# The opening stage of a two-layer diffusion trunk, in a new order: squares summed on DVE, five parts' modulation by rows of weights, seven product chains by parts and one at the end

## The chip, the cores and the metric

The kernel runs on one core of a Trainium2 chip, in float32 throughout; matrix products use float32r operands split into a high and a low part. The metric is the device time of one launch in microseconds (us), the median of several runs. "PE" is TensorE, "DVE" VectorE, "ACT" ScalarE, "POOL" GpSimd and "SP" the engine that issues most loads.

## The reference

Two layers over 256 latent tokens and 256 context tokens of width 1024. Each sub-layer first normalises and modulates with a shift and a scale that come from the conditioning vectors; the first is a SwiGLU over all 512 tokens:

```
silu_c, silu_cc = silu(c), silu(c_ctx)
m  = silu_c  @ w_mod[0] + b_mod[0]          # 9 x 1024: shift, scale, gate, ...
mc = silu_cc @ w_mod[0] + b_mod[0]          # the same for context tokens
h  = rms_norm(x, g) * (1 + scale) + shift
x  = x + 0.5 * gate * ((silu(a) * b) @ w2),   a, b = split(h @ w13)
... token mixing (attention and pooling), SwiGLU, layer 2: SwiGLU, gMLP, SwiGLU
```

Only the part up to `h @ w13` of the first SwiGLU is touched here.

## The kernel before

Everything is stored transposed: a tile has 128 features on partitions and tokens along the columns. `X` holds 8 parts of 128 features (k = 0 to 7), each 512 columns: 256 latent tokens, then 256 context tokens. A product in full precision is `mm3`: three matmuls, low weights with the high activations `AH`, high weights with `AH`, high weights with `AL`. `split` makes the pair: ACT casts the high part, DVE subtracts to get the low one.

The opening is `start()`. It runs the first four of the SwiGLU's 22 blocks of hidden features (f = 0 to 3, each with halves a and b, so eight chains in eight PSUM banks) part by part: for one part k, all eight chains get their three products, 8 x 3 x 8 = 192 products in all. So they can begin when one part is normalised and its weights are there, long before all modulation vectors are known. After it `ffn` goes on with block 4, whose weights come by `load_w`, whole blocks at a time.

For part k the kernel needs shift and scale of that part for both token kinds. They come in two ways:
- by reduction: a tile `wm` (128x1024, 0.5 MB) of transposed weights is multiplied on DVE with the broadcast conditioning vector `cc` and summed along the columns (`use_mod`, line L80); two tiles and two token kinds make four reductions a part; `finish_mod` adds the bias and makes `gs` = gain x (1 + scale);
- by rows: TensorE multiplies the conditioning columns with plain weight rows (`by_rows`, L697) into a row of results, ACT copies it, and narrow matmuls (L704) turn it into columns. Before the change the last `NR` = 3 parts go this way, all three in one block ahead of the first product.

The parts are taken in the order 0, 5, 1, 6, 2, 7, 3, 4. Part 0's four reductions come first; parts 1 to 4 are reduced beside the products.

Also in the opening, before: `cc` is made by 16 matmuls of a broadcast column with the identity (L665), copied by ACT (L667). The mean square of each token is summed on TensorE: ACT squares a part (L679), a matmul with `ones` adds it (L680), ACT takes the root (L681) and DVE the reciprocal of all 512 columns at once (L685), then `sa` = X times it (L721), ACT applies scale and shift (L724), and `split` makes `AH` and `AL`.

The tile framework sorts instructions of each engine by its own priorities, except those that are pinned with `tc.keep_in_program_order`; each engine runs its list strictly in order. SP's queue of loads is a list of the same kind. A tile name with `bufs=n` has n buffers, and a load into one waits until its last reader is through.

Of the kernel before, what the change touches and what calls it, by code (L numbers as in the profile page):

```python
# [16 lines left out]
P = 128  # L17
D = 1024
# [4 lines left out]
NH = NF // 2  # L23
EPS = 1e-6
NMOD = 72
NR = 3
WINDOWS = (2, 4, 8, 16)
ATTN_SCALE = 0.125

# [6 lines left out]
def trunk(ctx: ExitStack, tc: tile.TileContext, I, out):  # L36
# [47 lines left out]
    def finish_mod(layer, j, n=1, ks=slice(0, NK)):  # L84
# [7 lines left out]
        V.tensor_tensor(out=m, in0=m, in1=b.broadcast_to([P, ns, n, nk]), op=ALU.add)  # L92
        sub, kind = (j + n - 1) // 3, (j + n - 1) % 3
        last = m[:, :, n - 1]
        if kind == 1:
            g0 = C_NG + (layer * 3 + sub) * NK
            g = par[:, g0 + ks.start:g0 + ks.stop].unsqueeze(1).broadcast_to([P, ns, nk])
            V.scalar_tensor_tensor(out=gs[:, st, sub, ks], in0=last, scalar=1.0, in1=g,
                                   op0=ALU.add, op1=ALU.mult)
        if kind == 2:  # L100
            V.tensor_scalar(gate[:, st, sub, ks], last, 1.0 if j == 5 else 0.5, None, ALU.mult)
# [20 lines left out]
            run_mods(1)  # L122


    def load_w(src, n, pin=lambda ins: ins):
# [3 lines left out]
        nc.sync.dma_start(out=raw[:, :n], in_=src)  # L129
# [85 lines left out]
    def ffn(fi, layer, sub, n, mods, after, started=()):  # L215

        defer = n == T
        with tc.tile_pool(name=f"ffn{fi}", bufs=1) as fp:
            HH = fp.tile([P, NH, 2 * T], F32R, name="HH")
            HL = fp.tile([P, NH, 2 * T], F32R, name="HL")  # L220
            for half in range(2):
                hc = half * T if n == T else 0
                for fl in range(NH):
# [1 line left out]
                    if f < len(started):  # L225
                        ps = started[f]
                    else:
                        hi, lo = load_w(I["w13"][fi, f], 2048)
# [409 lines left out]

    def start():
        ng = 4  # L640
        order = (0, 5, 1, 6, 2, 7, 3, 4)
        with tc.tile_pool(name="start", bufs=1) as sp:
            def get_raw(k):
                raw = sp.tile([P, ng, 2 * P], F32, name="raw4", bufs=2)
                nc.sync.dma_start(out=raw, in_=I["w13"][0, 0:ng, :, k * 2 * P:(k + 1) * 2 * P]
                                  .rearrange("f p c -> p f c"))
                return raw

            cT = sp.tile([P, 2, NK], F32, name="cT")
            nc.sync.dma_start(out=cT, in_=I["cT"])  # L650
            nc.sync.dma_start(out=ident, in_=I["ident"])
            wm = {(0, 0): load_mod(0, 0, nc.sync)}
            for k in range(0, NK, 2):
                nc.sync.dma_start(out=X[:, k:k + 2], in_=I["xc"][:, k:k + 2])
            wm[0, 1] = load_mod(0, 1, nc.sync)
            S.activation(out=cT, in_=cT, func=AF.Silu)

            S.activation(out=rb[:, 0:1], in_=cT[:, 0, 0:1], func=AF.Sqrt, scale=0.0, bias=epsb)

            for st in range(2):  # L660
                for h in range(2):
                    ps = bank()
                    for k4 in range(4):
                        k = 4 * h + k4
                        PE.matmul(ps[:, k4 * P:k4 * P + P], cT[:, st, k:k + 1].broadcast_to([P, P]),  # L665
                                  ident, start=True, stop=True)
                    S.copy(cc[:, st, h * 512:h * 512 + 512], ps)  # L667
            nc.sync.dma_start(out=par, in_=I["par"])
            wn = [wpool.tile([P, 2, 2 * NR * P], F32, name=n, bufs=3 if i > 1 else 2)
                  for i, n in enumerate(("raw", "raw", "whi", "wlo"))]  # L670
            for i in range(4):
                nc.sync.dma_start(out=wn[i], in_=I["w_modr"][:, 2 * i:2 * i + 2])
            raws = {0: get_raw(0)}
            wm.update({(1, h): load_mod(0, 2 + h, nc.sync) for h in range(2)})
            raws[order[1]] = get_raw(order[1])
            ps = bank()
            for k in range(NK):
                sq = tmp.tile([P, 2 * T], F32, name="sq", bufs=2)
                S.activation(out=sq, in_=X[:, k], func=AF.Square)  # L679
                PE.matmul(ps, ones, sq, start=k == 0, stop=k == NK - 1)  # L680
            S.activation(out=rb, in_=ps, func=AF.Sqrt, scale=1.0 / D, bias=epsb)  # L681
            for h in range(2):
                use_mod(0, h, wm[0, h])
            finish_mod(0, 0, 2, slice(0, 1))
            V.reciprocal(rb, rb)  # L685
            sh = sp.tile([P, NK, ng - 2, 2 * P], F32R, name="sh")
            sl = sp.tile([P, NK, ng - 2, 2 * P], F32R, name="sl")
            wh, wl = ([wpool.tile([P, NK, 2 * P], F32R, name=n, bufs=3) for _ in range(2)]
                      for n in ("whi", "wlo"))

            def by_rows():

                row = sp.tile([2, 2 * NR * P], F32, name="row")
                ps = [bank() for _ in range(2)]
                for k in range(NK):
                    for j in range(2):
                        PE.matmul(ps[j][0:2, :NR * P], cT[:, :, k],  # L697
                                  wn[k // 2][:, k % 2, j * NR * P:(j + 1) * NR * P],
                                  start=k == 0, stop=k == NK - 1)
                for j in range(2):  # L700
                    S.copy(row[:, j * NR * P:(j + 1) * NR * P], ps[j][0:2, :NR * P])
                ps = bank()
                for i in range(2 * NR):
                    PE.matmul(ps[:, 2 * i:2 * i + 2], row[:, i * P:i * P + P], ident[0:2, 0:2],  # L704
                              start=True, stop=True)
                for st in range(2):
                    V.tensor_copy(mod[:, st, :16].rearrange("p (j k) -> p j k", j=2)[:, :, NK - NR:],
                                  ps[:, 0:4 * NR].rearrange("p (j k s) -> p s j k", j=2, k=NR)[:, st])
                finish_mod(0, 0, 2, slice(NK - NR, NK))

            by_rows()
            pss = [[bank(), bank()] for _ in range(ng)]
            nxt = 1
            for i, k in enumerate(order):
                raw = raws.get(k) or get_raw(k)
                split(sh[:, k], sl[:, k], raw[:, :2])
                split(wh[0][:, k], wl[0][:, k], raw[:, 2])
                split(wh[1][:, k], wl[1][:, k], raw[:, 3])
                xr = tmp.tile([P, 2 * T], F32, name="sa", bufs=2)
                h = tmp.tile([P, 2 * T], F32, name="h32", bufs=2)  # L720
                V.tensor_tensor(out=xr, in0=X[:, k], in1=rb, op=ALU.mult)  # L721
                for st in range(2):
                    ts = slice(st * T, st * T + T)
                    S.activation(out=h[:, ts], in_=xr[:, ts], func=AF.Identity,  # L724
                                 scale=gs[:, st, 0, k:k + 1], bias=mod[:, st, k:k + 1])
                if nxt < NK - NR and i in (0, 2, 4, 5):
                    for j in range(2):
                        use_mod(0, 2 * nxt + j, wm.get((nxt, j)) or
                                load_mod(0, 2 * nxt + j, nc.sync), tc.keep_in_program_order)
                    finish_mod(0, 0, 2, slice(nxt, nxt + 1))  # L730
                    nxt += 1
                split(AH[:, k, :2 * T], AL[:, k, :2 * T], h)

                def products(f, k, first, last):
                    for ab in range(2):
                        cs = slice(ab * P, ab * P + P)
                        w = (sh[:, k, f, cs], sl[:, k, f, cs]) if f < 2 else \
                            (wh[f - 2][:, k, cs], wl[f - 2][:, k, cs])
                        mm3(pss[f][ab], *w, AH[:, k, :2 * T], AL[:, k, :2 * T], first, last)

                for f in range(ng):
                    products(f, k, i == 0, i == NK - 1)
        return pss


# [14 lines left out]
def _pack(x, c, ctx, c_ctx, w_mod, b_mod, norm_g, ffn_w13, ffn_w2, w_in_a, qk_norm_g, pool_w,  # L760
# [5 lines left out]
    r["cT"] = ac(np.stack([c[0], c_ctx]).reshape(2, NK, P).transpose(2, 0, 1))  # L766
    r["w_modr"] = ac(w_mod[0][:, :2 * D].reshape(NK, P, 2, NK, P)[:, :, :, NK - NR:]
                     .transpose(1, 0, 2, 3, 4)).reshape(P, NK, 2 * NR * P)
# [70 lines left out]
```

## Time and profile before

| | us |
|---|---|
| runs | 1141.17, 1141.91, 1142.41; median 1141.91 |
| the profiled execution | 1142.17, of it the span of the core 1140.4 |
| TensorE busy | 1132.2 (99% of the span), 7696 matmul passes |
| DVE / ACT busy | 863.6 / 522.0 |
| TensorE busy in the first 27.8 us | 24.49, before the first product |

In the rows that are shown below, a timeline row is: start, duration, engine, line, operation, output<-inputs, shape, count, and in brackets the engine's idle time before it with what ended it. A row of waits is: who waited for whom, us in total, times, longest. A row of groups ends with busy us, mean ns of one, and idle time before. A row of a stretch is: from:to, length, then busy us and count for PE, weight loads, DVE, ACT and POOL (or PE alone), the granted clock of TensorE, the DMA engines' share and GB/s. A row of one source line gives count, minimum, median and maximum in ns, first and last start, and the forms with their counts.

### The profile page before, as it was taken

What the parts mean: (1) busy time and instruction counts of PE and PEld (TensorE: products, weight loads), DVE (VectorE), ACT (ScalarE), POOL (GpSimd) and SP (SyncE); (2) the same over time, 40 slices, a digit from 0 to 9 for tenths busy, and PEclk for the clock granted to TensorE, in tenths of its full rate; (3) what the DMA queues carried; (4) which work ended last, traced back from release to release, by engine and by line L of the source; (5) the groups of instructions that cost most, each with busy time, mean ns of one, the idle gap of its engine ahead of it and who ended that gap; (6) DMA issues with size and microseconds to landing.
All of it is one profiled execution on the core that took longest, in us unless ns stands there. A gap on an engine that the chain in (4) does not pass through costs nothing.

```text
span 1140.4 us, 19165 instructions
## 1 busy us (share of the span) xinstructions
PE 1132.2 (99%) x7696; PEld 1033.9 (91%) x7696; DVE 863.6 (76%) x1582; ACT 522.0 (46%) x816; POOL 68.4 (6%) x140
## 2 busy tenths in 40 slices
PE   8999999999999999999999999999999999999998
PEld 4888888888888897899999999999999899999998
DVE  5967787878789979777778887656667788756663
ACT  5552212223223357664335456435445866434442
POOL 0000111122222200000000000000000000000000
PEclk9999999999999999999999999999999999999999
DMA  8844656788888850556687566456447536546543
GB/s 323 310 148 156 197 186 234 279 282 325 294 297 306 305 196 11 222 172 223 212 305 264 187 219 218 161 167 219 174 143 257 185 114 219 176 154 237 178 143 114
DMA packets 52408, 242.72 MB, mean 213 GB/s; under 512 B 5600, under 2 KB 11488, under 8 KB 38880
## 3 DMA queue, kind: packets, MB, share of 16 engines
q1 hardware_dynamic: 33888, 174.39, 43.4%
q0 software_dynamic: 18432, 67.12, 17.4%
q8 instruction: 60, 0.98, 0.4%
q14 instruction: 28, 0.23, 0.1%
HBM read 240.44 MB, written 1.05 MB: 212 GB/s over the span
## 4 chain that ended last, share of the span: by engine, by line
PE 97%; DVE 1%; ACT 1%; DMA 1%; issue 0%; SPq 0%; DVEq 0%; ACTq 0%
PE ps L148 30%; PE ps L149 30%; PE ps L150 30%; PE ps L697 1%; PE ps L618 1%; PE ps L619 1%; PE ps L617 1%; PE ps L680 1%; PE ps L665 1%; DMA raw<-in_w_out_a 0%; ACT whi L153 0%; PE ps L501 0%; PE ps L469 0%; DVE st L473 0%; PE ps L172 0%; ACT pe L477 0%
## 5 line engine op out<-in xcount | busy, mean ns | idle before, releaser
L148 PE MATMUL ps<-AH,wlo 128*128 128x258 f32 (+2 forms) x1664 | 507.1, 305 | 0.3 <-ACT AH L153 0.3
L149 PE MATMUL ps<-AH,whi 128*128 128x258 f32 (+2 forms) x1664 | 506.6, 305 | 0.0
L150 PE MATMUL ps<-AL,whi 128*128 128x258 f32 (+2 forms) x1664 | 505.5, 305 | 0.0
L153 ACT CAST whi<-raw 128x1024 fp32r<-128x1024 f32 (+2 forms) x354 | 313.7, 921 | 363.7 <-PE ps L150 260.3
L154 DVE TENSOR_TENSOR wlo<-raw,whi 128x1024 fp32r<-128x1024 f32 (+2 forms) x354 | 367.6, 1064 | 54.4 <-ACT whi L153 53.4
L148 PEld LDWEIGHTS ps<-AH,wlo 128*128 128x128 f32 x1664 | 316.3, 190 | 16.1 <-issue 1.1
L149 PEld LDWEIGHTS ps<-AH,whi 128*128 128x128 f32 x1664 | 314.3, 189 | 14.7 <-issue 0.5
L150 PEld LDWEIGHTS ps<-AL,whi 128*128 128x128 f32 x1664 | 313.4, 189 | 14.5 <-issue 0.2
L150 PE MATMUL ps<-HL,whi 128*128 128x256 f32 (+1 forms) x704 | 218.0, 310 | 0.0
L149 PE MATMUL ps<-HH,whi 128*128 128x256 f32 (+1 forms) x704 | 218.0, 310 | 0.0
L148 PE MATMUL ps<-HH,wlo 128*128 128x256 f32 (+1 forms) x704 | 218.0, 310 | 0.0
L80 DVE CUSTOM_DVE_ANT_0 wm<-wm,cc 128x1024 f32<-128x1024 f32 x138 | 164.7, 1219 | 6.1 <-DMA wm<-in_w_mod 5.0
L148 PEld LDWEIGHTS ps<-HH,wlo 128*128 128x128 f32 x704 | 132.5, 188 | 7.8
L150 PEld LDWEIGHTS ps<-HL,whi 128*128 128x128 f32 x704 | 132.5, 188 | 7.7
L149 PEld LDWEIGHTS ps<-HH,whi 128*128 128x128 f32 x704 | 132.6, 188 | 7.7
L72 POOL DMA_DIRECT2D wm<-in_w_mod x128 | 67.7, 529 | 546.2 <-DVE mod L80 508.6
L206 ACT ACTIVATE sa<-sa,cb 128x256 f32<-128x256 f32 x66 | 33.6, 510 | 119.7 <-DVE sa L205 116.4
L246 DVE SCALAR_TENSOR_TENSOR X<-ps,gate,X 128x256 f32<-128x256 f32 x64 | 30.9, 482 | 48.0 <-PE ps L150 47.9
L204 DVE COPY cb<-ps 128x1 f32<-128x1 f32 x66 | 10.3, 155 | 72.8 <-PE ps L150 72.7
L212 DVE TENSOR_TENSOR h<-ps,sa 128x512 f32<-128x512 f32 x22 | 15.2, 692 | 43.4 <-PE ps L150 34.2
L80 DVE CUSTOM_DVE_ANT_0 junk<-wm,cc 128x1024 bf16<-128x1024 f32 x34 | 41.4, 1218 | 8.6 <-ACT cc L667 7.2
L154 DVE TENSOR_TENSOR HL<-h,HH 128x256 fp32r<-128x256 f32 (+1 forms) x88 | 42.3, 485 | 0.0
(162 smaller groups left out, 705.3 us busy)
## 6 DMA issues: line engine op xcount, KB each, us to landing
raw<-in_w SPq DMA_DIRECT2D x84, 1024.0 KB, 4.9
wm<-in_w_mod POOLq DMA_DIRECT2D x128, 512.0 KB, 5.0
raw<-in_w SPq DMA_DIRECT2D x64, 704.0 KB, 4.1
wm<-in_w_mod SPq DMA_DIRECT2D x10, 512.0 KB, 6.4
raw<-in_w_in_a SPq DMA_DIRECT2D x5, 1024.0 KB, 7.8
raw<-in_w SPq DMA_DIRECT2D x8, 512.0 KB, 5.3
raw<-in_w_out_a SPq DMA_DIRECT2D x4, 1024.0 KB, 5.0
raw<-in_w_in_cu SPq DMA_DIRECT2D x4, 1024.0 KB, 4.8
```

Of the source, the lines that this page charges most:

```text
L72: eng.dma_start(out=w, in_=I["w_mod"][layer, i])
L80: pin(V.tensor_tensor_reduce(out=res, in0=w, in1=cc[:, st, :], scale=1.0, scalar=0.0, op0=ALU.mult, op1=ALU.add, accum_out=mod[:, 2 * laye ...
L148: PE.matmul(ps, wl, xh, start=first, stop=False)
L149: PE.matmul(ps, wh, xh, start=False, stop=False)
L150: PE.matmul(ps, wh, xl, start=False, stop=last)
L153: S.copy(hi, src)
L154: pin(V.tensor_tensor(out=lo, in0=src, in1=hi.bitcast(F32), op=ALU.subtract))
L206: S.activation(out=sa[:, :T], in_=sa[:, :T], func=AF.Silu, bias=cb[:, 0:1])
L212: V.tensor_tensor(out=h32[:, :n], in0=ps[1][:, :n], in1=sa[:, :n], op=ALU.mult)
L246: V.scalar_tensor_tensor(out=X[:, m, :T], in0=ps[:, :T], scalar=gate[:, 2 * layer, sub, m:m + 1], in1=X[:, m, :T], op0=ALU.mult, op1=ALU.add)
L617: PE.matmul(ps[b], AL[:, k, ts], hi[:, ws], start=(k == 0), stop=False)
L618: PE.matmul(ps[b], AH[:, k, ts], hi[:, ws], start=False, stop=False)
```

## The change

Only the opening changes, and with it the packing of its inputs.
- The conditioning columns, with a small selector `sel`, come in one load `cs`; X is loaded first, in five pieces, with `wm` behind it. All loads of the opening are pinned in program order.
- `cc`: DVE multiplies the identity with the broadcast columns into a diagonal tile, and four 512-column matmuls with `ones` spread it; DVE copies one token kind's half, ACT the other's.
- Squares: ACT squares, DVE adds them into `acc` (`square_acc`), and two 256-column matmuls with `ones` sum over partitions at the end. Root and reciprocal are made by token half.
- The queue: a one-column ACT copy into the next rows' buffer makes SP hold that load, and all behind it, until ACT has come to part 5 of X.
- By rows now go five parts, `ROWS` = 3 to 7, one at a time: 8 matmuls with 32 stationary columns (2 real, the others zero) in four column groups of the array, partitions 32g to 32g + 31 of the bank; a row copy; two narrow matmuls with `sel`, which also add the four groups up. The first block stands ahead of the products, the others between the products of the part before.
- The order is 3, 4, 0, 5, 1, 6, 2, 7. Parts 0, 1 and 2 are reduced on DVE, one part ahead. The first part is done in token halves of 256 columns.
- Seven chains go by parts; the eighth (f = 3, half b) is done for all parts at the end, since the rows need a bank.
- `load_w` pins the loads of blocks 4 and 5. `raw4` has three buffers in place of two.

```diff
+ROWS = (3, 4, 5, 6, 7)
...
-        order = (0, 5, 1, 6, 2, 7, 3, 4)
+        order = (3, 4, 0, 5, 1, 6, 2, 7)
+        jobs = {1: 0, 2: 1, 4: 2}
...
+            diag = cc.rearrange("p s (k c) -> p s k c", k=NK)
+            bc = [bank() for _ in range(4)]
             for st in range(2):
+                V.tensor_tensor(out=diag[:, st], in0=ident.unsqueeze(1).broadcast_to([P, NK, P]),
+                                in1=c32[:, :, st:st + 1].broadcast_to([P, NK, P]), op=ALU.mult)
                 for h in range(2):
-                    ps = bank()
-                    for k4 in range(4):
-                        k = 4 * h + k4
-                        PE.matmul(ps[:, k4 * P:k4 * P + P], cT[:, st, k:k + 1].broadcast_to([P, P]),
-                                  ident, start=True, stop=True)
-                    S.copy(cc[:, st, h * 512:h * 512 + 512], ps)
+                    PE.matmul(bc[2 * st + h], ones, diag[:, st, 4 * h:4 * h + 4],
+                              start=True, stop=True)
...
+            for k in range(NK):
+                square_acc(k, 2 * T)
+                if k in (4, 5):
+                    V.tensor_copy(cc[:, 0, k % 2 * 512:k % 2 * 512 + 512], bc[k - 4])
+                if k == 5:
+                    pin(S.copy(rows[4][:, 0, 0:1], X[:, k, 0:1]))
+            for st in range(2):
+                ts = slice(st * T, st * T + T)
+                PE.matmul(ps[:, ts], ones, acc[:, ts], start=True, stop=True)
...
+            def by_rows(k):
+                w = rows.pop(k)
+                for kt in range(NK):
+                    g = kt % 4
+                    pin(PE.matmul(rw[32 * g:32 * g + 32, :2 * P], c32[:, kt], w[:, kt],
+                                  start=kt < 4, stop=kt >= 4))
+                row = sp.tile([P, 2 * P], F32, name="row", bufs=2)
+                pin(S.copy(row, rw[:, :2 * P]))
+                for j in range(2):
+                    PE.matmul(rw[:, 2 * P + 2 * j:2 * P + 2 * j + 2], row[:, j * P:j * P + P], sel,
+                              start=True, stop=True)
+                finish_mod(0, 0, 2, slice(k, k + 1),
+                           rw[:, 2 * P:2 * P + 4].rearrange("p (j s) -> p s j", j=2).unsqueeze(3))
...
+                if i == 0:
+                    for ts in halves:
+                        if ts.start:
+                            pin(V.reciprocal(rb[:, ts], rb[:, ts]))
+                            subs(pin)
+                            rest(halves[0])
+                        pin(V.tensor_tensor(out=xr[:, ts], in0=X[:, k, ts], in1=rb[:, ts],
+                                            op=ALU.mult))
+                        if ts.start == 0:
+                            casts(pin)
+                        normed(ts, AH[:, k, ts])
+                        normed(ts, h[:, ts])
+                    rest(halves[1])
...
+                else:
+                    for f, ab in todo:
+                        if ahead is not None and (f, ab) == (1, 0):
+                            by_rows(ahead)
+                        mm3(pss[f][ab], *tile(f, ab), AH[:, k, :2 * T], AL[:, k, :2 * T], False,
+                            i == NK - 1)
             ps = bank()
             for k in range(NK):
...
+                mm3(ps, *tile(ng - 1, 1, k), AH[:, k, :2 * T], AL[:, k, :2 * T], k == 0, k == NK - 1)
```

The built order shows it at three places. In its rows ISA is a reduction (L80 before, L81 after) and the short read that follows it; `sl` and `wlo` are low weights, `AL` low activations, and the numbers on `raw` and `h` tell parts apart. First DVE, from the reciprocal to the first low parts. Before:

```order
L685 RECIPROCAL rb<-rb 128x512
L721 TENSOR_TENSOR sa<-X,rb 128x512 x3
L154 TENSOR_TENSOR AL<-h_227,AH 128x512
L154 TENSOR_TENSOR sl<-raw_131,sh 128x512
L154 TENSOR_TENSOR wlo<-raw_131,whi 128x256 x2
```

The reciprocal was one operation of 512 columns, with all three low parts behind it. Now, on the same engine:

```order
L722 RECIPROCAL rb<-rb 128x256
L93 TENSOR_TENSOR mod<-ps,par 128x2x2
L100 SCALAR_TENSOR_TENSOR gs<-mod,par 128x2
L782 TENSOR_TENSOR sa<-X,rb 128x256
L779 RECIPROCAL rb<-rb 128x256
L764 TENSOR_TENSOR sl<-raw_97,sh 128x512
L764 TENSOR_TENSOR wlo<-raw_97,whi 128x256 x2
L772 TENSOR_TENSOR AL<-h_188,AH 128x256
```

The second half's reciprocal and the weights' subtractions now stand ahead of the first half's `AL`. Second, DVE beside the first products. Before, from the first part's weights on:

```order
L154 TENSOR_TENSOR wlo<-raw_131,whi 128x256 x2
L80 ISA junk,mod<-wm,cc 128x1024
L80 ISA mod 128x1
L80 ISA wm,mod<-wm,cc 128x1024
L80 ISA mod 128x1
L707 COPY mod<-ps 128x2x3 x2
L80 ISA junk,mod<-wm,cc 128x1024
L80 ISA mod 128x1
L92 TENSOR_TENSOR mod<-mod,par 128x2x2x3
L154 TENSOR_TENSOR sl<-raw_137,sh 128x512
```

The reductions there are those of part 1, the third in its order. Now, from the low activations of part 0, the third part, to `gs` of part 5, the fourth:

```order
L156 TENSOR_TENSOR AL<-h_313,AH 128x512
L81 ISA junk,mod<-wm,cc 128x1024
L81 ISA mod 128x1
L81 ISA wm,mod<-wm,cc 128x1024
L81 ISA mod 128x1
L81 ISA junk,mod<-wm,cc 128x1024
L81 ISA mod 128x1
L93 TENSOR_TENSOR mod<-ps,par 128x2x2
L81 ISA wm,mod<-wm,cc 128x1024
L81 ISA mod 128x1
L100 SCALAR_TENSOR_TENSOR gs<-mod,par 128x2
L764 TENSOR_TENSOR sl<-raw_204,sh 128x512
```

`gs` of part 5 stands behind all four reductions of part 1. (The four reductions of part 0 stand in the same way between `AL` of part 4 and `gs` of part 0.) Third TensorE. Before, the start of the products:

```order
L680 MATMUL ps<-sq,ones 128x512 x8
L697 MATMUL ps<-raw,cT 2x384 x8
L697 MATMUL ps<-whi,cT 2x384 x4
L697 MATMUL ps<-wlo,cT 2x384 x4
L704 MATMUL ps<-ident,row 128x2 x3
L148 MATMUL ps<-AH,sl 128x512
```

All rows (L697) stood ahead of the first product. Now (`c_99` is the 32-column conditioning tile, L730 the rows' matmuls, L735 the narrow ones, L825 the products in halves):

```order
L710 MATMUL ps<-acc,ones 128x256 x2
L730 MATMUL ps<-raw,c_99 32x256 x8
L735 MATMUL ps<-cs,row 128x2 x2
L825 MATMUL ps<-AH,sh 128x256 x4
L825 MATMUL ps<-AH,whi 128x256 x3
L825 MATMUL ps<-AL,sh 128x256 x4
L825 MATMUL ps<-AL,whi 128x256 x3
L825 MATMUL ps<-AH,sl 128x256 x4
L825 MATMUL ps<-AH,wlo 128x256 x3
L730 MATMUL ps<-raw,c_99 32x256 x8
L825 MATMUL ps<-AH,sh 128x256 x4
L735 MATMUL ps<-cs,row 128x2 x2
```

One rows block is ahead of the products and the next already between them.

More of the change, by code (lines that the diff above doesn't have):

```diff
@@ L128, in load_w @@
         lo = wpool.tile([P, 2048], F32R, name="wlo", bufs=3)
-        nc.sync.dma_start(out=raw[:, :n], in_=src)
+        dma_pin(nc.sync.dma_start(out=raw[:, :n], in_=src))
         for c in (slice(0, n // 2), slice(n // 2, n)):
@@ L646, in get_raw @@
                                   .rearrange("f p c -> p f c"))
                 return raw
[L649 to L656, printed above, removed]
@@ new lines, in start @@
+            sync = InOrder(nc.sync)
+            cs = sp.tile([P, 2 * NK + 2], F32, name="cs")
+            sync.dma_start(out=cs, in_=I["cs"])
+            sel = cs[:, 2 * NK:]
+            sync.dma_start(out=ident, in_=I["ident"])
+            for ks in (slice(0, 2), slice(2, 4), slice(4, 6), slice(6, 7), slice(7, 8)):
+                sync.dma_start(out=X[:, ks], in_=I["xc"][:, ks])
+            sync.dma_start(out=par, in_=I["par"])
+            rows, raws, wm = {}, {}, {}
+            get_rows(3)
@@ L671, in start @@
[L671 to L675, printed above, removed]
+                    PE.matmul(bc[2 * st + h], ones, diag[:, st, 4 * h:4 * h + 4],
+                              start=True, stop=True)
+            ps = bank()
+            rw = bank()
+            pin = tc.keep_in_program_order
@@ new lines, in start @@
+            get_rows(4, load=False)
+            for k in range(NK):
[7 more added lines that the diff above has]
+                PE.matmul(ps[:, ts], ones, acc[:, ts], start=True, stop=True)
+            for st in range(2):
+                ts = slice(st * T, st * T + T)
+                pin(S.activation(out=rb[:, ts], in_=ps[:, ts], func=AF.Sqrt, scale=1.0 / D,
+                                 bias=epsb))
@@ L676, in start @@
             ps = bank()
             for k in range(NK):
[L678 to L742, printed above, removed]
```

113 lines of the change are left out of this document (99 added, 14 removed).

## The prediction

> **What bounds the kernel now.** First the share of the chain of work that ended last, then TensorE's own waits over the whole span, then three stretches: up to the first product, the opening's products, and the stretch after them.
>
> ```profile
> PE 97%; DVE 1%; ACT 1%; DMA 1%; issue 0%; SPq 0%; DVEq 0%; ACTq 0%
> ```
> ```profile
> PE ps L665 <- DMA ident<-in_ident: 3.3, 1, 3.3
> PE ps L501 <- ACT pt L493: 0.9, 2, 0.5
> PE ps L469 <- ACT wm L153: 0.4, 1, 0.4
> PE ps L148 <- ACT AH L153: 0.3, 1, 0.3
> ```
> ```profile
> 0.00:27.80 27.80, 24.49 (x86) 11.75 (x86) 15.12 (x24) 14.87 (x26) 0.20 (x4) 1.00 0.86 323
> 27.80:73.40 45.60, 45.60 (x200) 36.94 (x201) 38.63 (x80) 26.40 (x52) 2.24 (x4) 1.00 0.71 245
> 73.40:151.00 77.60, 77.60 (x337) 62.88 (x336) 57.95 (x86) 23.15 (x32) 6.87 (x13) 1.00 0.53 177
> ```
>
> TensorE is the bound: it carries 97% of the chain and waits under 5 us in 1140. From 27.8 us on it is busy without a break (third number of a row). So the change is worth exactly what it does to one instant: when TensorE has done the opening's 192 products of 512 columns and the six narrow ones beside them (the 200 of the second row, within the window's edges) and starts the first product of block 4. Whatever is earlier or later there is passed on to the end, because no later stretch has slack on TensorE. The timeline of TensorE gives that instant and what stands ahead of the products:
>
> ```profile
> 3.31 6.15 PE L665 MATMUL ps<-ident,cT 128*128 128x128 f32 x32 [3.31 <-DMA ident<-in_ident]
> 9.30 7.42 PE L680 MATMUL ps<-sq,ones 128*128 128x512 f32 x16
> 16.65 5.32 PE L697 MATMUL ps<-raw,cT 128*2 128x384 f32 x16
> 27.06 0.82 PE L704 MATMUL ps<-ident,row 2*128 2x2 f32 x6
> 27.82 0.50 PE L148 MATMUL ps<-AH,sl 128*128 128x512 f32 x1
> ...
> 73.07 0.39 PE L150 MATMUL ps<-AL,whi 128*128 128x512 f32 x1
> 73.30 0.40 PE L148 MATMUL ps<-AH,wlo 128*128 128x512 f32 x1
> ```
>
> Products begin at 27.82 and block 4 at 73.30; a product takes 0.23 from start to start, so 192 are 44.5. An f32 matmul is two passes: L697's 32 passes (16 of them in this row) of 384 columns go (27.06 - 16.65)/32 = 0.325 us apart, so a pass of 256 columns is 0.217. 27.82 is nearly all TensorE's own preparatory work, and this the change cuts. The sum is made against the profiled execution (1142.17 us, span 1140.4) and carried over to the median, 1141.91, which is 0.26 lower.
>
> **Step 1: up to the first product.** What X allows is read from the queue, since SP issues its next load when a piece of X has landed, and by equal bytes: after cT and ident the old queue has 0.52 MB of wm before X, the new one starts with X.
>
> ```profile
> 8.92 0.33 SPq L672 DMA_DIRECT2D wlo<-in_w_modr  x1
> 10.15 0.38 SPq L645 DMA_DIRECT2D raw<-in_w  x1
> ```
> ```profile
> 12.73 1.22 DVE L80 CUSTOM_DVE_ANT_0 junk<-wm,cc 128x1024 bf16<-128x1024 f32 x1 [1.38 <-DMA wm<-in_w_mod]
> ```
>
> wm and two pieces had landed by 8.92, so X's third piece now lands about then, the last (2.1 MB) at 10.15. With X, wm twice: 3.15 MB by 12.73; the first rows (1.05 MB behind X and par) land near 13. The queue's hold waits for ACT to reach part 5 of X, at about 10.1, when 1.6 MB are still queued, so it leaves no gap. The costs of single instructions come from the groups of the first 75 us, and from two lines for the 256-column forms:
>
> ```profile
> L724 ACT ACTIVATE h<-sa,mod,gs 128x256 f32<-128x256 f32 x16 | 8.9, 595 | 9.4 <-DVE sa L721 6.8 <-DVE gs L98 2.4
> L153 ACT CAST AH<-h 128x512 fp32r<-128x512 f32 x8 | 5.0, 620 | 0.2
> L679 ACT ACTIVATE sq<-X 128x512 f32<-128x512 f32 x8 | 4.9, 628 | 2.3 <-PE ps L680 1.7 <-DMA X<-in_xc 0.6
> L667 ACT COPY cc<-ps 128x512 f32<-128x512 f32 x4 | 2.3, 581 | 1.6 <-PE ps L665 1.6
> L92 DVE TENSOR_TENSOR mod<-mod,par 128x4 f32<-128x4 f32 x5 | 0.8, 160 | 0.0
> L98 DVE SCALAR_TENSOR_TENSOR gs<-mod,par 128x2 f32<-128x2 f32 x5 | 0.8, 156 | 0.0
> ```
> ```profile
> L173 ACT ACTIVATE rb<-ps,epsb x5: 474/476/690, 410.7 to 952.7; 128x256 f32<-128x256 f32 x4, 128x512 f32<-128x512 f32 x1
> L174 DVE RECIPROCAL rb<-rb x5: 1753/1754/3353, 411.4 to 953.2; 128x256 f32<-128x256 f32 x4, 128x512 f32<-128x512 f32 x1
> L504 ACT COPY hn<-ps x4: 365/373/419, 451.2 to 468.6; 128x256 f32<-128x256 f32 x4
> ```
> ```profile
> 23.98 0.68 DVE L154 TENSOR_TENSOR sl<-raw,sh 128x512 fp32r<-128x512 f32 x1
> 24.58 0.75 DVE L154 TENSOR_TENSOR wlo<-raw,whi 128x256 fp32r<-128x256 f32 x2
> 25.25 1.22 DVE L80 CUSTOM_DVE_ANT_0 junk<-wm,cc 128x1024 bf16<-128x1024 f32 x1
> 26.39 0.08 DVE L80 DVE_READ_ACCUMULATOR2_ANT mod<- 128x1 f32 x1
> 26.51 1.23 DVE L80 CUSTOM_DVE_ANT_0 wm<-wm,cc 128x1024 f32<-128x1024 f32 x1
> ```
>
> From start to start a 512-column DVE operation is 0.60, a 256-column one 0.33, a reduction over a mod tile 1.26 (25.25 to 26.51); ACT's overlap by some 0.1. X's third piece at 8.92: a square (0.63), then four additions, for which ACT and DVE take turns through two sq tiles (0.63 + 0.68 and two handovers for two, 0.74 each) and their end: 12.6. Two sums, four passes of 256 columns and the drain: 13.7. ACT then does two square roots (0.38 each), two cc copies (0.49 each), and only then the row copy (0.37): 15.8; the rows' matmuls lie beside this. Two narrow transposes (four passes, 0.45 with the drain of L704's row above in proportion): 16.4 to 16.6. DVE's sum and gs: 17.0; sa 0.42, ACT's AH 0.60: products start at **18.0**, 9.8 us earlier than 27.82. The two diagonals on DVE (1.2 each, by the 1024-column reduction) and the four matmuls on them end by 11, even at the half speed of rival 4's rows, and are hidden behind X and the additions; so are the constants that now go into one tile.
>
> **Step 2: what is now between the products.** Four rows blocks. The nearest rows for matmuls that use a part of the array's columns (64 of 128, two groups):
>
> ```profile
> 449.08 1.46 PE L501 MATMUL ps<-pt,VV 128*64 128x256 f32 x11
> 450.17 0.38 PE L377 MATMUL ps<-ident,ri 128*64 128x128 f32 x2
> 450.37 0.38 PE L501 MATMUL ps<-pt,VV 128*64 128x256 f32 x1
> ```
>
> From the first start to the eleventh, ten steps of 0.217 would be 2.17; they took 1.46 - 0.38 = 1.08, so two groups run side by side. And two L377 passes, which stand behind the last L501 in the program, start before it (450.17 against 450.37): a group that waits doesn't hold up the other. So I take four groups of 32 side by side: a block of 16 passes is four deep, 0.95. Bounds: 0.86 (four passes) to 3.46 (none beside another). The change between whole array and part of it has its own price:
>
> ```profile
> 434.00 0.28 PE L149 MATMUL ps<-AH,whi 128*128 128x258 f32 x1
> 434.21 0.49 PE L469 MATMUL ps<-wm 64*128 64x512 f32 x2
> 434.64 0.39 PE L150 MATMUL ps<-AL,whi 128*128 128x258 f32 x1
> ```
>
> A 258-column product passes in 0.12 (0.23 for 512) and the pair in 0.23, yet the next start 0.21 and 0.43 later: 0.1 and 0.2, so 0.3 to 0.35 a visit. That is nearest, bounds 0 and 0.4. Narrow transposes: 0.45. A rows block is thus 0.95 + 0.35 + 0.45 = 1.75 us of TensorE; the old 10.4 us of L697 are gone for it.
>
> The Trainium skill, "TensorE: Matmul & The Clock Gate", Part 3, says of packed matmuls that they start and end strictly in program order. By that rule the second pass of a group would hold up all behind it, and only neighbours would overlap: nine steps, 1.94. The trace disagrees (450.17 before 450.37); by the rule the sum would be 3 us higher.
>
> **Step 3: DVE and ACT in front of the products.** Read along the new order, with the prices above.
> - DVE from sa's start at 17.0: 0.33, half a reciprocal 1.67, sl 0.60, two wlo 0.67, AL 0.42: 20.7. TensorE has seven short products (0.8) until 18.9 and waits **1.8**. Then 14 short ones (1.6), the rows of part 4 (1.3), four short ones beside the row copy, transposes 0.45: 24.7; DVE's sum and gs: 25.05; ACT two h (0.5 each) and the cast 0.62: part 4 starts at 26.9, **0.4** after TensorE was free.
> - Part 4 has 21 products, 4.87, to 31.8. DVE: AL until 27.5, four reductions 5.04, sum and gs 0.4: 33.05. ACT 1.75: part 0 starts at 34.9. **3.1** of waiting.
> - TensorE: 4.87 and a rows block, free at 41.5. DVE: AL until 35.5, four reductions with the rows' sum between, gs of part 5 behind the fourth: 40.7. ACT: two h of part 5, one of part 1 queued before the cast, the cast: 43.0. **1.5**.
> - From there each part's tiles are ready in time: five parts 24.35, two rows blocks 3.5, the eighth chain 24 products 5.57: block 4 starts at **76.4**.
>
> 76.4 - 73.30 = **+3.1 us**: 9.8 won at the start, 7.0 given to four rows blocks, 6.8 to waits, less the 0.9 that the old second group of transposes took among the products. Block 4's weights are cast and subtracted (four operations of 1024 columns, by the reduction's row some 1.2 each) while the eighth chain runs, 5.6 us; without that cover block 4 would be late by what is left of them. SP's loads of the opening are the same 14.9 MB in another order, by the shapes; POOL's order is as it was. Forecast 1141.91 + 3.1 = **1145.0**, own range 1144.0 to 1146.0. No change means within 0.2%, 2.3 us.
>
> **Rivals.**
> 1. *Not slower: entering and leaving the column groups is free* (weights already loaded behind the running product). Place: both ends of the three rows blocks on the path (parts 4, 6, 7; part 5's is in a wait). Price 3 x 0.35 = 1.05; +2.05, 1144.0, no change. It decides from 0.27 a block. For it: the row above is K-tiled, not column-tiled. Against: it shows the gap. The Trainium skill, "TensorEngine Tiling (Array Packing)", Key Properties, says that a change of tiling mode drains the array, as the row does.
> 2. *Groups overlap in pairs only*: 1.94 a block, +1.0 on three: +6.1, 1148.0. For it: the trace shows only two groups at once.
> 3. *No overlap at 32 columns*: +2.5 on three, 1.0 on part 5's, 1.7 on the first: +13.3, 1155.
> 4. *The array slows.* The first stretch shows two speeds of one instruction at a granted clock of 1.00:
>
> ```profile
> 3.30:8.10 4.80, 4.79 (x22) 1.00 0.95 349
> 8.20:9.25 1.05, 1.05 (x11) 1.00 1.03 367
> ```
>
> 22 passes in 4.8 us, then 11 in 1.05: half speed for the first 4.8. TensorE now idles from 11 to 20.7 with only 3.5 us of work in it; if half speed returns there, 14 short products, rows and transposes up to 24.7 double: up to +3.1, +4 to +6, about 1147. Against: no single gap is over 2.2 us. The Trainium skill's first-named page, Part 1, says that a window of 3.4 us of idling brings the half rate back; no run here shows a return.
> 5. *Faster*: waits of step 3 would have to fall from 6.8 to under 1.5. The order on DVE is fixed and each wait is made of rows above; I know of no row for it.
>
> **How the numbers follow.** Forecast 0.42 (0.08 of it under 2.3 us), rival 1 0.23, rival 2 0.13, rival 4 0.08, rival 3 0.03; unseen 0.11, of it 0.08 faster. Slower 0.34 + 0.13 + 0.08 + 0.03 + 0.03 = 0.61, no change 0.08 + 0.23 = 0.31, faster 0.08. The range takes rivals 1, 2 and 4 in: 1142.3 to 1148.5.
>
> **What would show it.** First product at 18.0 (17.5 to 18.5); TensorE waits on DVE AL 1.8 near 20.7, on ACT AH 3.1 near 35 and 1.5 near 43; 16 passes of a rows block in 1.0 (1.9: rival 2; 3.5: rival 3); block 4's first product at 76.4. The forecast is wrong if the waits at 35 and 43 are absent, or if TensorE idles anywhere after 80.

## The result and the profile after

| | median us | runs | lowest to highest | ratio to before, 95% interval |
|---|---|---|---|---|
| before | 1142.16 | 4 | 1141.17 to 1142.62 | |
| changed | 1148.66 | 4 | 1148.01 to 1151.85 | 1.0064 [1.0043, 1.0084] |
| changed, measured again (last experiment) | 1148.05 | 5 | 1146.89 to 1148.77 | 1.0052 [1.0039, 1.0066] |

The change makes the kernel 6 us slower, where 3.1 were forecast. The first profile is of the longest run, 1151.85, with a span of 1150.1. The chain and TensorE's waits, first:

```profile
PE 91%; DVE 4%; DMA 2%; ACT 2%; issue 1%; SPq 0%; DVEq 0%; ACTq 0%
```
```profile
PE ps L694 <- DVE cc L691: 4.6, 1, 4.6
PE ps L150 <- ACT AH L155: 4.0, 4, 2.6
PE ps L710 <- DVE acc L165: 3.3, 1, 3.3
PE ps L825 <- ACT AH L768: 1.5, 1, 1.5
PE ps L620 <- DVE AL L156: 0.9, 1, 0.9
...
PE ps L825 <- DVE AL L772: 0.7, 1, 0.7
PE ps L735 <- ACT row L733: 0.5, 1, 0.5
```

Before, TensorE waited 3.3 us in the opening for the identity's load, and hardly after that. Now TensorE waits for the diagonal (L694), the additions (L710), AH, AL and the row copy. The places that the prediction named, in TensorE's timeline of the same run:

```profile
16.32 1.94 PE L730 MATMUL ps<-raw,c 128*32 128x256 f32 x16
...
21.23 1.22 PE L825 MATMUL ps<-AH,sh 128*128 128x256 f32 x4 [1.48 <-ACT AH L768]
...
23.81 1.22 PE L825 MATMUL ps<-AL,sh 128*128 128x256 f32 x4 [0.72 <-DVE AL L772]
...
27.09 1.07 PE L730 MATMUL ps<-raw,c 128*32 128x256 f32 x16
...
39.30 0.50 PE L150 MATMUL ps<-AH,sl 128*128 128x512 f32 x1 [2.62 <-ACT AH L155]
...
40.93 1.94 PE L730 MATMUL ps<-whi,c 128*32 128x256 f32 x16
...
48.56 0.50 PE L150 MATMUL ps<-AH,sl 128*128 128x512 f32 x1 [0.95 <-ACT AH L155]
...
81.85 0.40 PE L150 MATMUL ps<-AH,wlo 128*128 128x512 f32 x1
```

The last row is block 4's first product, 8.55 after the 73.30 of before; from there to 380 us nearly all instructions of ACT and DVE are about 8.55 behind those of before, so the opening is where most of the time went. (Near 880 another 1.0 is lost in this run, in the second mixer, where TensorE waits 0.9: the row L620 above. In the profile of the last experiment, of the same kernel, that wait is 0.5; that of the kernel without the hold has none. Why it comes stays open.) The waits stand in the places that were forecast. What the forecast lacks shows in one pair of rows: the same 16 passes of a rows block take 1.07 us at 27.09, and 1.94 at 16.32 and 40.93. The granted clock, in stretches of 3.4 us from 10.1 on (from:to, length, TensorE busy, instructions, clock, DMA share, GB/s):

```profile
10.10:13.50 3.40, 0.88 (x2) 1.00 1.01 403
13.50:16.90 3.40, 2.59 (x12) 0.50 1.02 403
16.90:20.30 3.40, 2.36 (x20) 0.50 1.05 391
20.30:23.70 3.40, 1.86 (x7) 0.50 0.47 158
23.70:27.10 3.40, 3.29 (x15) 0.50 0.76 275
...
37.40:40.80 3.40, 1.50 (x6) 1.00 0.29 98
40.80:44.20 3.40, 3.40 (x20) 0.50 1.00 348
```

From 13.5 to 27.1 and from 40.8 to 44.2 TensorE ran at half clock. Before the change the view has 1.00 in every stretch that the prediction shows. In the first of them that is no measurement: the trace's list of clock changes begins at 8.2 us there, the view prints 1.00 for all that lies ahead of it, and up to 8.1 the prediction's own rows show matmuls at half speed.

### The profile page after: what moved, and what is told of

It reads as the page before. It is cut to its first block, busy times and chain, and to the rows that moved or that the text cites. A ratio compares the mean times of both kernels' runs of the same rounds, so it can differ in the third digit from the quotient of the medians.

```text
span 1150.1 us, 19262 instructions
## 1 busy us (share of the span) xinstructions
PE 1130.0 (98%) x7737; PEld 1033.5 (90%) x7737; DVE 864.2 (75%) x1583; ACT 521.6 (45%) x821; POOL 68.4 (6%) x140
## 3 DMA queue, kind: packets, MB, share of 16 engines
q1 hardware_dynamic: 33600, 174.39, 42.8%
## 4 chain that ended last, share of the span: by engine, by line
PE 91%; DVE 4%; DMA 2%; ACT 2%; issue 1%; SPq 0%; DVEq 0%; ACTq 0%
PE ps L150 29%; PE ps L152 29%; PE ps L151 29%; DMA raw<-in_w_in_cv 1%; DVE wlo L156 1%; ACT whi L155 1%; PE ps L621 1%; PE ps L620 1%; PE ps L622 1%; PE ps L730 1%; DMA X<-in_xc 1%; DMA raw<-in_w_in_cu 0%; DVE acc L165 0%; DMA raw<-in_w_out_a 0%; PE ps L825 0%
## 5 line engine op out<-in xcount | busy, mean ns | idle before, releaser
L155 ACT CAST whi<-raw 128x1024 fp32r<-128x1024 f32 (+1 forms) x338 | 307.7, 945 | 364.9 <-PE ps L152 260.6
L156 DVE TENSOR_TENSOR wlo<-raw,whi 128x1024 fp32r<-128x1024 f32 (+1 forms) x338 | 361.4, 1094 | 62.6 <-ACT whi L155 61.9
L81 DVE CUSTOM_DVE_ANT_0 wm<-wm,cc 128x1024 f32<-128x1024 f32 x134 | 159.8, 1219 | 5.4 <-DMA wm<-in_w_mod 4.8
L155 ACT CAST HH<-h 128x256 fp32r<-128x256 f32 (+1 forms) x88 | 39.9, 454 | 3.4 <-DVE h L214 2.3
```

Source lines behind the costliest of these rows:

```text
L81: pin(V.tensor_tensor_reduce(out=res, in0=w, in1=cc[:, st, :], scale=1.0, scalar=0.0, op0=ALU.mult, op1=ALU.add, accum_out=mod[:, 2 * laye ...
L155: S.copy(hi, src)
L156: pin(V.tensor_tensor(out=lo, in0=src, in1=hi.bitcast(F32), op=ALU.subtract))
```

## The experiments

Nine kernels, five to eleven runs each. Where a median of the changed kernel is compared, it is the 1148.05 of the last run unless said otherwise.

**Fill TensorE's waits.** Small matmuls that nobody reads keep it busy.

```diff
+            def fill(n, to=pss[0][0]):
+                for _ in range(n):
+                    pin(PE.matmul(to[:, 384:512], ones, ident, start=True, stop=True))
+            fill(12)                       # behind the cc matmuls
...
+                if k == order[0]: fill(4)  # behind the first rows
...
             by_rows(order[0])
+            fill(5)
...
+                            if j == 1 and ts.start == 0: fill(8, rw)
...
+                    if i == 1: fill(10, rw)  # behind part 4's products
```

> The changed kernel with 39 small f32 matmuls (128 columns, two passes each) on TensorE where it waits: 12 behind the cc matmuls, 4 behind the first rows, 5 behind the first narrow ones, 8 behind the first seven products, 10 behind part 4's products. Their results are overwritten or never read. Theory A (the halved clock costs): in the profile of the change the sums took 2.07 instead of about 1.0, the first narrow matmuls 1.01 instead of 0.50, the 14 short products from 23.81 3.28 instead of 1.6, the rows and products from 40.93 some 1.3 too long, 4.4 us together in a run with five windows of half clock and about 2.6 in one with three. The granted clock comes back to 1.00 throughout and the time falls by 2.5 to 4.4 us, to 1144.5 to 1146.2. Rival B (the half clock lies beside waits for DVE and ACT anyway): the clock is 1.00, the time within 1 us of the changed kernel's, 1148 to 1149.5.

Measured: 1145.80 (1145.03 to 1146.39), 2.9 below the changed kernel's first median and 2.25 below its second, ratio to before 1.0033 [1.0020, 1.0045]; clock 0.999 to 1.000 in all five runs (the last 1.4 us of its profile, when TensorE is done, lie at half clock, so 0.999 needs none in the opening). Its profile:

```profile
10.40:13.80 3.40, 3.40 (x28) 1.00 1.06 410
13.80:17.20 3.40, 3.32 (x33) 1.00 1.02 379
17.20:20.60 3.40, 3.15 (x27) 1.00 1.03 389
20.60:24.00 3.40, 3.40 (x38) 1.00 0.85 229
```
```profile
18.46 0.74 PE L836 MATMUL ps<-AH,sh 128*128 128x256 f32 x4 [0.26 <-ACT AH L777]
...
21.09 0.72 PE L836 MATMUL ps<-AL,sh 128*128 128x256 f32 x4
...
22.93 1.07 PE L737 MATMUL ps<-raw,c 128*32 128x256 f32 x16
...
27.41 0.50 PE L150 MATMUL ps<-AH,sl 128*128 128x512 f32 x1 [0.20 <-ACT AH L155]
...
76.35 0.40 PE L150 MATMUL ps<-AH,wlo 128*128 128x512 f32 x1
```

More work on TensorE, and less time: the idle stretches cost more than their own length. Block 4 starts at 76.35, 3.05 after before: without the half clock the opening is as long as the prediction's sum made it (76.4). The time as a whole is 3.85 above before (1141.95 beside these runs); in the profile some 0.5 of that comes behind 880 us. Theory A holds, rival B falls.

**Another order of parts.** Rows of part 5 directly after part 4, two reductions beside each part, and the loads moved to match.

```diff
-        order = (3, 4, 0, 5, 1, 6, 2, 7)
-        jobs = {1: 0, 2: 1, 4: 2}
+        order = (3, 4, 5, 0, 6, 1, 7, 2)
+        jobs = {1: (0, 0), 2: (0, 1), 3: (1, 0), 4: (1, 1), 5: (2, 0), 6: (2, 1)}
```

> The changed kernel with the parts in the order 3, 4, 5, 0, 6, 1, 7, 2 and two reductions beside each part in place of four beside every second one; loads moved to match; nothing else. Theory A: the waits of 2.6 us before part 0 and 0.95 before part 5 go (under 0.5 left in all), and with the first of them the second stretch of half clock (1.3): 3.0 to 4.7 us less, about 1144.5 to 1145.7; the first stretch of half clock (about 13.5 to 27) stays. Rival C (DVE is the bound in the opening, the waits only move): TensorE waits as long elsewhere before 85 us, time within 1 us of 1148.7.

Measured: 1144.31 (11 runs, 1143.54 to 1146.19), ratio 1.0024 [1.0015, 1.0033]: 3.7 less than the changed kernel, where 3.0 to 4.7 were expected, and as much as the two waits that it takes away (2.62 and 1.12 in the last profile below). TensorE's waits on ACT's casts of AH:

```profile
PE ps L150 <- ACT AH L155: 0.4, 2, 0.3
```

4.0 became 0.4, and the waits came back nowhere else. The clock was 0.994 to 0.997: the first stretches of half clock stayed (12.8 to 16.2 and 19.6 to 26.4 in its profile), none came later. Theory A holds, rival C falls.

**Copies of `cc` out of the way.** DVE's two behind the last addition, ACT's two ahead of the roots.

```diff
-                if k in (4, 5):
-                    V.tensor_copy(cc[:, 0, k % 2 * 512:k % 2 * 512 + 512], bc[k - 4])
...
+            for b in range(2):
+                pin(V.tensor_copy(cc[:, 0, b * 512:b * 512 + 512], bc[b]))
+            for b in range(2):
+                pin(S.copy(cc[:, 1, b * 512:b * 512 + 512], bc[2 + b]))
```

> The changed kernel with DVE's two cc copies behind its last addition and ACT's two cc copies ahead of the roots (while ACT waits for the sums). Theory A: the last addition ends 0.6 earlier, the row copy waits only for the rows' matmuls; first product 0.6 to 0.8 earlier, time 0.6 to 0.8 us lower at the same number of half-clock windows. Rival D (the late landing of X alone sets the end of the additions): first product within 0.2 of 21.2, no change.

Measured: 1148.23 (1146.79 to 1149.04): no gain that can be told. In the profile, of its shortest run, the first product came at 17.02, 1.2 earlier than the 18.26 that the changed kernel's second profile shows below; the other four runs had clocks of 0.994 and 0.995, where the changed kernel's five had 0.995 to 0.997. At the same clock the runs are faster than those of the changed kernel in the table below: 0.6 at 0.997 and 0.7 at 0.995 (not at 0.994, one run each). So the start was shortened, as theory A has it for an equal number of half-clock stretches, and the lower clock of most runs took the gain back; that the shorter start brings the lower clock is argued from these few runs, not shown. Rival D falls.

**No hold of the queue.**

```diff
-                if k == 5:
-                    pin(S.copy(rows[4][:, 0, 0:1], X[:, k, 0:1]))
```

> The changed kernel without the one-column copy that holds the queue. Theory A: the rows of part 4 are needed at 27, nine us after they land, and X is at the head of the queue: no change, within 0.7 us of the changed kernel. Rival E (loads in flight share the DMA engines, so the second piece of X landed at 8.5 with 1.8 MB moved): X's last piece lands 0.5 to 1.0 later than 11.07 and the time rises by as much.

Measured: 1148.09 (6 runs, 1147.05 to 1151.57), the changed kernel's time. The hold is worth nothing either way; rival E falls.

**Order, copies and 16 fills together, and another DVE order.** Beside the order, the copies and the fills (8, 2 and 6), the weights' subtractions and the first AL now stand ahead of the second half's reciprocal:

```diff
                         if ts.start:
-                            pin(V.reciprocal(rb[:, ts], rb[:, ts]))
                             subs(pin)
                             rest(halves[0])
+                            pin(V.reciprocal(rb[:, ts], rb[:, ts]))
```

> The changed kernel with four things together: the order 3, 4, 5, 0, 6, 1, 7, 2 with two reductions a part, the cc copies in ACT's and DVE's wait for the sums, the first half's AL (with the weights' subtractions) ahead of the second half's reciprocal on DVE, and 16 small f32 matmuls in the opening waits (8 behind the cc matmuls, 2 behind the first rows, 6 behind the narrow ones). Theory A (half clock, waits behind reductions, and the 1.1 of cc copies on ACT make up the loss): granted clock 1.00, first product near 17.0, part 4 near 24.2, no wait over 0.6 from then on, time 1139 to 1141, faster than the kernel before by 0.1 to 0.25%. Rival F (TensorE has no more to win in the opening, each wait removed comes back elsewhere): 1142 to 1144.

Measured: 1138.42 (6 runs, 1138.26 to 1138.58), ratio to before 0.9969 [0.9958, 0.9980]: 3.65 us faster than the kernel before, 9.6 faster than the changed one, and faster than the 1139 to 1141 that were expected. Its places:

```profile
17.06 0.73 PE L835 MATMUL ps<-AH,sh 128*128 128x256 f32 x4
...
18.04 0.74 PE L835 MATMUL ps<-AL,sh 128*128 128x256 f32 x4
...
69.52 0.40 PE L150 MATMUL ps<-AH,wlo 128*128 128x512 f32 x1
```
```profile
PE ps L150 <- ACT AH L155: 0.8, 2, 0.6
```

First product at 17.06 as expected, no wait for AL, no wait over 0.6 in the products, block 4 at 69.52: 3.78 earlier than before. Rival F falls.

**The same without fills.** The diff is against the fifth kernel.

```diff
-            fill(8)
...
-                if k == order[0]: fill(2)
...
-            fill(6)
```

> The same as the run before it, without the 16 small matmuls. Theory A: the idle stretch of 2 us or more ahead of the sums brings the half clock in most runs (granted clock 0.994 to 0.998), which costs 1.5 to 3 us: 1141.5 to 1143.5. Rival B (half clock hidden behind DVE and ACT): within 0.5 us of the run before it.

Measured: 1140.21 (11 runs, 1138.13 to 1141.95), ratio 0.9982 [0.9973, 0.9991]. The fills are worth 1.8 at the median, and above all they make the runs alike: a spread of 0.3 with them, 3.8 without. Its clock was 0.998 to 1.000, less half clock than expected, so the time is below the expected 1141.5 to 1143.5, and in the profiled run there was none ahead of block 4 (at 69.49). Two runs at 0.999 took 1141.1 and 1141.95, more than half clock alone can cost there; what else they waited for stays open. One at a time the order, AL first (below) and the copies were worth 3.7, 1.1 and nothing; together, without fills, 7.8. What is more than the sum goes with the higher clock (0.995 to 0.997 before); how it splits is not shown.

**Fill only the wait before part 0.**

```diff
+                    if i == 1: fill(8, rw)
```

> The changed kernel with 8 small f32 matmuls behind part 4's products alone, in the wait of 2.6 us before part 0. Theory A: the stretch of half clock that followed that wait (40.7 to 44.2 in the profile of the change) is gone, the first one (13.5 to 27) stays: clock 0.995 to 0.997, time 0.5 to 1.3 below the changed kernel, 1147.4 to 1148.2. Rival G (what halves the clock is not the idle stretch but a limit on the load, which comes after the loads of weights start again): the second stretch stays.

Measured: 1146.77 (1146.56 to 1147.33), 1.3 below the changed kernel and faster than the 1147.4 to 1148.2 that were expected; clock 0.997 in four of five runs. One stretch of half clock is left in its profile, 17.4 to 24.2, and none after the filled wait, though the loads go on as before. That speaks for theory A and against rival G; since the changed kernel's second profile has no second stretch either, the clocks of all runs carry this, not the one profile. More against G: the clock fell at 40.8 of the first profile after a stretch with the DMA at 0.29, and the filled kernel keeps 1.00 with it at 1.02 to 1.06.

**AL first alone.** The diff of the fifth run's fence; in both kernels ACT's making of AH and h in the first part is pinned in order too.

> The changed kernel with the weights' subtractions and the first half's AL ahead of the second half's reciprocal on DVE; nothing else. Theory A: the wait of TensorE for the first AL (0.7 at half clock) goes, the second half is 0.4 later on DVE but TensorE comes to it later still; first AL product 0.7 earlier: time 0.4 to 0.8 lower, 1147.8 to 1148.3. Rival H (the reciprocal, now behind, makes the second half late): 0 to 1 us slower.

Measured: 1146.99 (1146.77 to 1148.70), 1.06 below; at the same clock of 0.997 it is 0.5 (1146.9 against 1147.4), within the expected 0.4 to 0.8. TensorE no longer waits for AL; its only waits in the products are on AH. Rival H falls.

**The changed kernel again**, unedited.

> The changed kernel once more, unedited, beside the kernel before. If the lost time follows the stretches of half clock, runs with a mean clock of 0.997 or 0.996 take 1147 to 1148, of 0.995 or 0.994 1148.5 to 1149.5, of 0.993 near 1151, and the median falls between 1147.5 and 1149. In the profile the block-4 product starts 6 us later than before where X's last piece lands near 10 and 8 where it lands near 11; if time and clock don't go together here, the half clock is not what costs.

Measured: 1148.05, runs of 1146.89 to 1148.77. The table takes these five, the first four, and the six without the hold, whose median is the same:

| mean clock of the run | times, us | mean |
|---|---|---|
| 0.997 | 1146.89, 1147.05, 1147.09, 1147.73, 1148.05 | 1147.4 |
| 0.996 | 1147.82, 1148.01, 1148.05, 1148.37 | 1148.1 |
| 0.995 | 1148.77, 1149.28, 1149.41 | 1149.2 |
| 0.994 | 1148.36 | 1148.4 |
| 0.993 | 1151.57, 1151.85 | 1151.7 |

0.004 less clock is 0.008 x 1147 = 9.2 us more at half clock. That can cost half, 4.6 us; the table has 4.35. Not all of it is the clock, though: in the run of 1151.85 X also came 1.4 late (point 2 of the next section). From 0.997 to 0.995 it is 1.8 of at most 2.3. So most of the half clock lies on the path. From 0.997 to 1.000 the slope of 4.35 gives 3.3 less, 1144.1 (an estimate by extension, below all these runs); the filled kernel measured 1145.8, so that slope is too steep, or the fills cost something themselves. Time and clock go together as expected. Its profile, of the run of 1148.05, has block 4 5.04 after before, where 6 was expected:

```profile
18.26 0.74 PE L825 MATMUL ps<-AH,sh 128*128 128x256 f32 x4 [1.48 <-ACT AH L768]
...
20.83 1.22 PE L825 MATMUL ps<-AL,sh 128*128 128x256 f32 x4 [1.28 <-DVE AL L772]
...
24.12 1.87 PE L730 MATMUL ps<-raw,c 128*32 128x256 f32 x16
...
29.41 0.50 PE L150 MATMUL ps<-AH,sl 128*128 128x512 f32 x1 [0.18 <-ACT AH L155]
...
37.14 0.50 PE L150 MATMUL ps<-AH,sl 128*128 128x512 f32 x1 [2.62 <-ACT AH L155]
...
45.05 0.50 PE L150 MATMUL ps<-AH,sl 128*128 128x512 f32 x1 [1.12 <-ACT AH L155]
...
78.34 0.40 PE L150 MATMUL ps<-AH,wlo 128*128 128x512 f32 x1
```
```profile
15.60:19.00 3.40, 1.35 (x10) 1.00 1.07 392
19.00:22.40 3.40, 2.12 (x10) 0.50 0.84 282
22.40:25.80 3.40, 3.40 (x25) 0.50 1.01 386
...
32.60:36.00 3.40, 1.92 (x9) 1.00 0.48 188
```

## Why the prediction was wrong

The second profile of the changed kernel and the profile of the filled one (first experiment), set against the prediction's instants:

| | forecast | measured | stretch longer by | with fills | stretch longer by |
|---|---|---|---|---|---|
| first product | 18.0 | 18.26 | +0.26 | 18.46 | +0.46 |
| part 4 starts | 26.9 | 29.41 | +2.25 | 27.41 | +0.05 |
| part 0 starts | 34.9 | 37.14 | -0.27 | 35.14 | -0.27 |
| part 5 starts | 43.0 | 45.05 | -0.19 | 43.05 | -0.19 |
| block 4 starts | 76.4 | 78.34 | -0.11 | 76.35 | -0.10 |

1. **The step that failed is rival 4's dismissal**, the array slowing down: it had a chance of 0.08, and the sum has no term for it. In all fifteen runs of the table the clock was below 1, and the one stretch of the second profile that is off by more than 0.3 is the one in which it was halved, 19.0 to 25.8; with fills, at full clock, that stretch is off by 0.05. There the 14 short products behind AL take 3.29 us (20.83 to 24.12) where the filled kernel's take 1.84 (21.09 to 22.93), and the rows 1.87 where they take 1.07: 2.25 together. The place and the mechanism were named, and even the price of the smaller case (+3.1, and 1147 for the whole); the argument against it, "no single gap is over 2.2 us", was the error. The longest gap in the 3.4 us before the fall at 19.0 was 1.48. What preceded the falls was a stretch of 3.4 us in which TensorE was busy for 1.35 us (second profile), 0.88 and 1.50 (first). In that light the prediction's own numbers, 3.5 us of work from 11 to 20.7, spoke for it.
2. **Step 1 was right where X was on time, and the first profile hid that.** In the run of 1151.85 X came late: ACT waited for it ahead of the third square (first row), which it did not in the second profile. Then the additions on DVE, first in that run, then in the second profile:

```profile
8.52 1.15 ACT L164 ACTIVATE sq<-X 128x512 f32<-128x512 f32 x2 [1.91 <-DMA X<-in_xc]
```
```profile
11.19 3.07 DVE L165 TENSOR_TENSOR acc<-acc,sq 128x512 f32<-128x512 f32 x4
```
```profile
9.76 3.07 DVE L165 TENSOR_TENSOR acc<-acc,sq 128x512 f32<-128x512 f32 x4
```

   They end at 14.26 and 12.83 (forecast 12.6). An addition takes 0.77 there where 0.74 was reckoned, and a `cc` copy that the prediction had not put on the path stood ahead of them. Late X (1.4) and a longer half clock, 17.1 us for 6.8, set that run's 8.55 apart from the second one's 5.04; how much each costs there is not shown.
3. **Step 2 was right.** Between 54.68 and 57.48 of the first profile, products and a rows block with its narrow transposes, five products' steps of 0.23 leave 1.65 for the block, forecast 1.75:

```profile
54.68 0.39 PE L152 MATMUL ps<-AL,sh 128*128 128x512 f32 x1
54.99 1.07 PE L730 MATMUL ps<-wlo,c 128*32 128x256 f32 x16
...
56.80 0.50 PE L735 MATMUL ps<-cs,row 128*128 128x2 f32 x4
...
57.48 0.39 PE L151 MATMUL ps<-AH,sh 128*128 128x512 f32 x1
```

   Sixteen passes in 1.07 show four groups at once: rivals 2 and 3 (1.9 and 3.5) fall, and so does rival 1, which leaves out 0.35 and so has 1.4.
4. **Step 3 was right in places and slightly too large in size**: 1.28, 0.18, 2.62 and 1.12 against 1.8, 0.4, 3.1 and 1.5. Part of that is in the adding up: from the instants that it states, its terms give 26.7, 34.7 and 42.8 for parts 4, 0 and 5 in place of 26.9, 34.9 and 43.0, and so waits of 0.2, 2.9 and 1.3. The wait for AL is shorter because the seven products ahead of it ended later, at 19.56 in place of 18.9; AL itself came at 20.83, forecast 20.7. The reordered kernel, which loses the waits of 2.62 and 1.12, shows that these were what four reductions on DVE at a time cost.
5. The range was exceeded by 0.16 us at the first median; the 1148.05 of the run again lies in it. That makes the size no better: the medians are 6.5 and 6.2 above before. +3.1 is what is left of the opening when the half clock is taken out (3.05 with fills). The prediction also had whatever block 4 loses passed on to the end unchanged; in the second profile it is 5.04 at block 4 and about 5.7 behind 900 us, and TensorE's waits near 880, 0.9 and 0.5 in the two profiles, are the idling after 80 that the prediction named as a sign of being wrong.

The Trainium skill, "TensorE: Matmul & The Clock Gate", Part 1, which the prediction cited for this, has the clock gate look at a free-running window of some 3.4 us. The runs agree on that length: in seven profiles with half clock the stretches last 3.4, 6.8, 10.2 or 13.6 us to 0.1. The same part of the Trainium skill names an idle window as what halves the rate; here a window that was busy for less than half was enough.

## What to carry to other kernels

Where TensorE is the bound, a stretch in which it waits can cost more than its own length, when what follows runs at half clock (2.25 us here in the 6.8 us of the second profile): count its work in each 3.4 us ahead of dense work, not its longest gap. Some unread matmuls in such a wait are cheap insurance: 39 of them gained 2.25 us on the changed kernel, and 16 brought the spread of the best one from 3.8 us to 0.3. Moving work off a bounding engine pays only if the others deliver: of the 9.6 us between the changed and the best kernel, 7.8 came without fills, from the order on DVE and ACT with the same work on each, and from the higher clock that went with it.

## What the runs showed of the hardware

Stretches of 3.4 us in two more profiles, first of the kernel with the copies moved, then of the one with the single filled wait:

```profile
14.70:18.10 3.40, 1.69 (x11) 0.99 1.03 378
18.10:21.50 3.40, 1.92 (x10) 0.50 1.05 381
...
31.70:35.10 3.40, 1.64 (x8) 1.00 0.62 239
```
```profile
14.00:17.40 3.40, 1.65 (x21) 1.00 1.02 383
17.40:20.80 3.40, 1.86 (x7) 0.50 1.04 392
```

The clock fell after stretches of 3.4 us in which TensorE was busy for 0.88 to 1.69 us, and rose after ones in which it was busy for 3.11 (the kernel without the hold, 21.12 to 24.53) to 3.40; at half clock, stretches of 1.86 to 2.64 (the latter with AL first, 12.76 to 16.18) did not bring it back. At full clock, stretches of 1.70 and more were not followed by a fall. Below that it is not the busy time alone. Of stretches with 512-column matmuls only, 1.50 in the first profile was followed by a fall (1.48 from 37.37 to 40.78, the edges to 0.01), but 1.64 above was not, nor was 1.51 from 8.73 to 12.14 of the second profile; 1.65 and 1.69 with narrow matmuls in them were. Whether narrow matmuls count for less was not tried. Where the stretches begin differs from run to run, and with that and with the landing of X the time of one and the same kernel, by 5 us in the table.
